# Output projections in two halves of 512 tokens, later half first in the even layer, and the first MLP iteration taken product by product

## The chip, the cores and the metric

The kernel runs on one core of one Trainium2 chip. The metric is the device time of one execution in microseconds (us), the median of the runs. The profiled execution is one more execution of the same program, with every instruction recorded.

## The reference

A two-layer decoder trunk, one batch of 1024 tokens, model width 1024, all in float32. Each layer is a mixer and an MLP, each inside a sandwich of two RMS norms with a modulation computed from `c`:

```
h   = rms_norm(x) * (1 + scale) + shift
x   = x + gate * rms_norm(mixer(h))          # even: Mamba-2 heads | differential attention
h   = rms_norm(x) * (1 + scale) + shift      # odd:  retention | sliding-window attention
x   = x + gate * rms_norm(relu(h @ W1)**2 @ W2)
```

`mixer(h)` ends in an output projection: the concatenated head outputs (2048 columns in the even layer, 1536 in the odd one) times a weight matrix with 1024 columns. This projection, the norms behind it, and the start of `h @ W1` are what the change rearranges.

## The kernel before

Every float32 product is made of three TensorE (PE) matmuls: each operand is split into a high part (written by a cast on ScalarE, ACT) and a low part (the difference, written by VectorE, DVE). In names, `wh`/`wl` are the two parts of a weight tile, `hh`/`hl` those of the normalized input `hT`, `uh`/`ul` those of a projected activation. `split_w` makes a weight pair: the cast at L160, the subtraction at L162. Instructions are put on each engine by a scheduler of the build, so program text gives the dependences and priorities and the scheduler the order; once built, each engine's order is fixed, and an instruction that waits holds back all behind it on its engine. DMAs go out from SP's queue.

The four sub-layers are numbered s = 0 (even mixer), 1 (MLP), 2 (odd mixer), 3 (MLP). Tokens are eight tiles of 128 (`t` = 0 to 7); a *half* is four tiles, 512 tokens.

**Output projection** (`MixerOut`). The mixer's columns are taken in groups of 512: four groups in the even layer, three in the odd one, listed in `order`. For one group, `half` transposes the activations of one half of the tokens (tile `pyt`, L922), scales them on ACT (L929) and splits them on DVE (L930). `load_group` loads the group's weights (two DMAs of 1 MB into `raw`), splits them into four pairs, and lets `bg` start one or more background tasks. `out_unit` (L456 to L458) is one token tile by 512 output columns: twelve 128x512 matmuls into a bank of `pg`, then a copy (L463, first group) or an addition (L465) into `Y` on DVE. `__init__` does the first half of the tokens for the first two groups, while the heads of the mixer are still being computed. `finish` did the rest: the second half for groups 1 and 0, then all eight token tiles of each remaining group, and with the last group also the norm and residual of each tile (`post`, L383 and L388), the norm of the next sub-layer (`pre_norm`, L372) and the transposes into `hT[0]` (`hT_cols`, L425 to L429).

**Background tasks** (`bg`, queue `bgq`): the modulation vectors of later sub-layers. A task loads a piece of the modulation matrix (`mraw`, into the same ring of two `raw` buffers as the weights) and accumulates it on DVE (`macc`, L289); four of these end in `parts` (L210, L211).

**Even mixer, end.** The last of eight attention heads is computed in blocks of 128 queries, from the last block to the first. A block goes through PE (`psc`, L857), DVE (L1215, bias and maximum), ACT (L1218, exponential), DVE (L1223 to L1228), PE (`pat`, L1235, transposes), ACT or DVE (L1237), PE (`pav`, L1241), ACT (L1245), DVE (L133), GpSimd (POOL, L135) and DVE (`ys`, L1248).

**MLP, first matrix** (`ud` is its result). The product of a 2x2 block form is made with seven products instead of eight (operands `A[1]` to `A[7]`, weights `x11` to `x22`, sums and differences of them). Each product is two times twelve matmuls (L547 to L549). Iteration 0 of eight starts as soon as `hT[0]` (the first half of the tokens) is there: products 1 and 2 need nothing else. `second_half` then makes the other operands from `Y[4]` to `Y[7]`: 32 transposes (L564), ACT (L566, L568, L500) and DVE (L501, L570 to L574); then come products 4, 6, 7, 5, 3.

## Time and profile before

| | us |
|---|---|
| median of 3 runs | 3018.76 (3018.48 to 3020.44) |
| profiled execution, its own time | 3018.32 |
| its span (first to last instruction) | 3016.5 |
| outside the span | 1.8 |
| PE busy in the span | 2922.7 |
| DVE busy | 1978.0 |
| ACT busy | 1325.2 |
| POOL busy | 471.9 |

The sub-layers follow each other in the span: the even mixer ends its attention near 957, its output projection near 1088, where the first MLP begins; the odd mixer ends its output projection near 2364, where the second MLP begins. The mean granted clock of PE over the span is 0.988 of full speed.

### The profile page before, as it was taken

Reading aid. Unit: us, or ns where it says so; the run is one execution under the profiler, and the core shown is the slowest. Engines: PE = TensorE matmul, PEld = TensorE weight load, DVE = VectorE, ACT = ScalarE, POOL = GpSimd, SP = SyncE. Lnnn points to the kernel's source line nnn. Section 1 sums busy time; section 2 is a strip of 40 time slices with the busy share of each in tenths; the row PEclk is TensorE's granted clock in tenths of the full one; section 3 lists DMA queues with packets and bytes.
Section 4 is the critical chain, followed back from the end, with each engine's and each line's share of the span. In section 5 each row is a group of like instructions: output and inputs, shape, how many; then the busy total and the mean of one; then the engine's idle time right before and its main releaser. Section 6 shows DMA issues by size and latency. Waiting matters only on the chain.

```text
span 3016.5 us, 40087 instructions
## 1 busy us (share of the span) xinstructions
PE 2922.7 (97%) x15250; PEld 2465.3 (82%) x15250; DVE 1978.0 (66%) x3211; ACT 1325.2 (44%) x2359; POOL 471.9 (16%) x430
## 2 busy tenths in 40 slices
PE   8999999999999989999999989999999899999998
PEld 5888888898877867888888878989988678888887
DVE  5677875765686579876646845565454876666476
ACT  5343335555553264445333545432222644454343
POOL 0244532322200020000000232001101200000021
PEclk9999999999999999999999999999999999999999
DMA  6211211322142236646736542153242464476464
GB/s 216 75 55 50 90 43 50 109 66 67 55 149 97 72 123 229 217 158 242 281 126 233 190 131 64 33 172 102 81 154 77 147 199 149 151 268 232 146 231 160
DMA packets 269091, 413.60 MB, mean 137 GB/s; under 512 B 15721, under 2 KB 151522, under 8 KB 268002
## 3 DMA queue, kind: packets, MB, share of 16 engines
q1 hardware_dynamic: 268512, 410.92, 40.0%
q8 instruction: 120, 1.97, 0.3%
q14 instruction: 73, 0.60, 0.1%
q10 hardware_dynamic: 386, 0.11, 0.0%
HBM read 319.23 MB, written 91.75 MB: 136 GB/s over the span
## 4 chain that ended last, share of the span: by engine, by line
PE 85%; DVE 6%; DMA 4%; ACT 2%; issue 1%; POOL 1%; SPq 0%; POOLq 0%; DVEq 0%; ACTq 0%
PE pg L444 5%; PE pg L445 5%; PE pg L446 5%; PE pw L730 5%; PE pw L731 5%; PE pw L732 5%; PE pw L547 4%; PE pw L548 4%; PE pw L549 4%; PE pg L798 4%; PE pg L800 4%; PE pg L799 4%; PE pg L456 3%; PE pg L458 3%; PE pg L457 3%; PE pg L730 2%
## 5 line engine op out<-in xcount | busy, mean ns | idle before, releaser
L160 ACT CAST wh<-raw 128x1024 fp32r<-128x1024 f32 (+1 forms) x218 | 227.4, 1047 | 331.0 <-PE pw L548 104.5
L798 PE MATMUL pg<-wh,hh 128*128 128x256 f32 (+1 forms) x992 | 290.7, 293 | 11.2 <-DVE ms L133 6.0
L444 PE MATMUL pg<-hh,wh 128*128 128x512 f32 x736 | 293.0, 398 | 3.4 <-ACT wh L160 2.5
L446 PE MATMUL pg<-hh,wl 128*128 128x512 f32 x736 | 292.1, 397 | 0.3 <-DVE ms L133 0.3
L162 DVE TENSOR_TENSOR wl<-raw,wh 128x1024 fp32r<-128x1024 f32 (+1 forms) x162 | 199.3, 1233 | 141.0 <-ACT wh L160 138.9
L445 PE MATMUL pg<-hl,wh 128*128 128x512 f32 x736 | 291.1, 396 | 0.0
L800 PE MATMUL pg<-wh,hl 128*128 128x256 f32 (+1 forms) x992 | 286.2, 289 | 0.6 <-DVE hl L429 0.6
L799 PE MATMUL pg<-wl,hh 128*128 128x256 f32 (+1 forms) x992 | 285.0, 287 | 0.0
L500 ACT CAST u<-uraw 128x1024 fp32r<-128x1024 f32 x112 | 117.0, 1049 | 298.4 <-PE pw L731 177.0
L501 DVE TENSOR_TENSOR u<-uraw,u 128x1024 fp32r<-128x1024 f32 x112 | 141.0, 1261 | 152.0 <-ACT u L500 151.7
L731 PE MATMUL pw<-wl,u 128*128 128x512 f32 x608 | 240.3, 395 | 0.0
L730 PE MATMUL pw<-wh,u 128*128 128x512 f32 x608 | 240.1, 396 | 0.0
L732 PE MATMUL pw<-wh,u 128*128 128x512 f32 x608 | 239.4, 394 | 0.0
L135 POOL TENSOR_TENSOR rs<-ms,expo 128x1 f32<-128x1 f32 x160 | 106.9, 669 | 642.4 <-DVE ms L133 630.2
L798 PEld LDWEIGHTS pg<-wh,hh 128*128 128x128 f32 x992 | 191.7, 193 | 14.3 <-issue 8.1
L799 PEld LDWEIGHTS pg<-wl,hh 128*128 128x128 f32 x992 | 191.6, 193 | 1.9 <-issue 0.5
L800 PEld LDWEIGHTS pg<-wh,hl 128*128 128x128 f32 x992 | 191.1, 193 | 2.0 <-DVE hl L429 1.3
L456 PE MATMUL pg<-wh,u 128*128 128x512 f32 x448 | 181.9, 406 | 2.7 <-DVE u L930 2.1
L458 PE MATMUL pg<-wh,u 128*128 128x512 f32 x448 | 178.3, 398 | 0.0
L457 PE MATMUL pg<-wl,u 128*128 128x512 f32 x448 | 177.0, 395 | 0.0
L162 POOL TENSOR_TENSOR wl<-raw,wh 128x1024 fp32r<-128x1024 f32 x58 | 145.9, 2520 | 155.6 <-ACT wh L160 148.6
L444 PEld LDWEIGHTS pg<-hh,wh 128*128 128x128 f32 x736 | 139.1, 189 | 31.8 <-ACT wh L160 2.9
(456 smaller groups left out, 7237.0 us busy)
## 6 DMA issues: line engine op xcount, KB each, us to landing
x<-in_mlp_w_dram SPq DMA_DIRECT2D x128, 512.0 KB, 7.5
uraw<-ud SPq DMA_DIRECT2D x56, 1024.0 KB, 5.6
mraw<-in_mod_w_dram SPq DMA_DIRECT2D x64, 512.0 KB, 4.6
ud<-sums SPq DMA_DIRECT2D x48, 512.0 KB, 5.3
raw<-in_mlp_w_dram SPq DMA_DIRECT2D x18, 1024.0 KB, 6.0
raw<-in_e_w_in_dram SPq DMA_DIRECT2D x32, 512.0 KB, 3.9
ud<-c SPq DMA_DIRECT2D x64, 256.0 KB, 3.0
raw<-in_mlp_w_dram SPq DMA_DIRECT2D x28, 512.0 KB, 5.0
```

The lines of the kernel that those rows point to most:

```text
L162: lo_on[0].tensor_tensor(out=wl, in0=src, in1=wh.bitcast(F32), op=ALU.subtract)
L444: mm(ps, lhsT=wh[:, k], rhs=hh[:, k], start=(k == 0), stop=False)
L445: mm(ps, lhsT=wh[:, k], rhs=hl[:, k], start=False, stop=False)
L446: mm(ps, lhsT=wl[:, k], rhs=hh[:, k], start=False, stop=(k == 7))
L456: mm(ps, lhsT=uh[:, tl], rhs=wh[:, f % 2], start=(f == 0), stop=False)
L458: mm(ps, lhsT=ul[:, tl], rhs=wh[:, f % 2], start=False, stop=(f == 3))
L730: mm(ps[t], lhsT=uh[:, k, ts], rhs=wh[:, k], start=b, stop=False, **on)
L731: mm(ps[t], lhsT=uh[:, k, ts], rhs=wl[:, k], start=False, stop=False, **on)
L732: mm(ps[t], lhsT=ul[:, k, ts], rhs=wh[:, k], start=False, stop=e, **on)
L798: mm(ps[:, 0:n], lhsT=hh[:, k, tl], rhs=wh[:, i], start=(k == 0), stop=False)
L799: mm(ps[:, 0:n], lhsT=hh[:, k, tl], rhs=wl[:, i], start=False, stop=False)
L800: mm(ps[:, 0:n], lhsT=hl[:, k, tl], rhs=wh[:, i], start=False, stop=(k == 7))
```

## The change

`out_group` is gone; `finish` does the projections by halves:

- For groups 2 and up, only the first half of the tokens; tokens outside, column halves inside. Then all background tasks that are left are issued (`bg(len(bgq))`).
- Then the second half for all groups, from the last group down to 0. Beside these units, one step of `along` at a time does `post`, `pre_norm` and `hT_cols` for the first half. With group 0, `post` and `pre_norm` follow for each tile of the second half.
- Weights of a group that is needed twice, at a distance, are loaded and split twice: seven calls of `load_group` in place of five in the even layer, five in place of four in the odd one.
- In the even layer the first half is tokens 512 to 1023 (`real(t)` gives the tile's place in memory); the odd mixer turns its halves round.
- The transposed activations of `finish` in the even layer go to the bank pool `pt` instead of `pg`.

In the MLP's iteration 0, `second_half` is a generator of five steps. Its first step is held behind the last matmul of product 2 by `tc.issue_after`; each later step makes the operand of the next product. The order of the products is 4, 7, 6, 5, 3. One quarter (`a21`) is transposed twice, so that 48 transposes are made instead of 32.

```diff
+            def group(i):
+                return load_group(self.w, self.order[i] * 512)
-            room = (pg, "g") if self.s == 0 else (pt, "t")
-            for i in (1, 0):
-                nc.sync.dma_start(out=yr[:, i], in_=self.yd[self.order[i]][:, 4:8])
-                us = self.half(i, 1, [yr[:, i, t] for t in range(4)], u_tiles(), *room)
-                if i == 0:
-                    bg_n[0] = 2
-                    self.gb = load_group(self.w, self.order[0] * 512)
-                for cc in range(2):
-                    for t in range(4, 8):
-                        out_unit(yp, [None, us], self.gb, t, cc, i == 1)
-            n = len(self.order)
             for i in range(2, n):
                 bg_n[0] = 5
-                us = [self.half(i, hf, [yr[:, hf * 4 + t] for t in range(4)], u_tiles(), pt, "t") for hf in range(2)]
-                gb = load_group(self.w, self.order[i] * 512)
-                late = out_group(yp, us, gb, self.s, False, i == n - 1)
+                us = self.half(i, 0, [yr[:, t] for t in range(4)], u_tiles(), pt, "t")
+                self.gb = group(i)
+                for t in range(4):
+                    for cc in range(2):
+                        out_unit(yp, [us, None], self.gb, t, cc, False)
+            bg(len(bgq))
...
+            for i in reversed(range(n)):
...
+                us = self.half(i, 1, [yr[:, i % 2, t] for t in range(4)], u_tiles(), pt, "t")
+                gb = self.gb if i == n - 1 else group(i)
+                for t in range(4, 8):
+                    for cc in range(2):
+                        out_unit(yp, [None, us], gb, t, cc, i == n - 1)
+                        if step % 2 == 0 or n == 3:
+                            along(step if n == 3 else step // 2)
+                        step += 1
+                    if i == 0:
+                        x_new = post(yp, t, s)
+                        if s != sub_last:
+                            pre_norm(yp, t, x_new)
```

```diff
                 for g in range(2):
-                    product(pa[g], 2, w, g, False, True)
+                    last = product(pa[g], 2, w, g, False, True)
                     square_relu(c11[g], pa[g])
-                if it == 0:
-                    second_half()
...
+                more = second_half() if it == 0 else iter(range(5))
+                with tc.issue_after(last):
+                    next(more)
                 for g in range(2):
                     product(pe[g], 4, w, g, True, True)
```

How the orders moved, at three places (line numbers below are those of the kernel that is shown in each).

First, PE near the end of the even mixer: the last blocks of the last attention head. `psc_8916` is the last block's score tile, `pat` and `pav` its transposes and its product with `v`; L456 to L458 (L463 to L465 in the changed kernel) are matmuls of `out_unit`. Before:

```order
L1241 MATMUL pav<-v,aT 128x128 [waits DVE_49]
L1241 MATMUL pav<-v,aT 128x128 x2
L1235 MATMUL pat<-kmat,p 128x128 [waits DVE_49]
L1235 MATMUL pat<-kmat,p 128x128
L857 MATMUL psc_8916<-ks,qh 128x128 [waits Activation_49]
L858 MATMUL psc_8916<-ks,ql 128x128
L457 MATMUL pg<-wl,u 128x512
L458 MATMUL pg<-wh,u 128x512
L456 MATMUL pg<-wh,u 128x512 [waits DVE_49]
L457 MATMUL pg<-wl,u 128x512
L458 MATMUL pg<-wh,u 128x512
```

After the change, from the same score tile to the first unit of the next group:

```order
L881 MATMUL psc_8916<-ks,qh 128x128 [waits Activation_49]
L882 MATMUL psc_8916<-ks,ql 128x128
L1303 MATMUL pav<-v,aT 128x128 [waits DVE_49]
L1303 MATMUL pav<-v,aT 128x128 x2
L1297 MATMUL pat<-kmat,p 128x128 [waits DVE_49]
L1297 MATMUL pat<-kmat,p 128x128
L1303 MATMUL pav<-v,aT 128x128 [waits Activation_49]
L1303 MATMUL pav<-v,aT 128x128
L1297 MATMUL pat<-kmat,p 128x128 [waits DVE_49]
L1303 MATMUL pav<-v,aT 128x128 [waits Activation_49]
L948 MATMUL pyt<-kmat,yr 128x128 [waits DMAHW5_49,DVE_49]
L948 MATMUL pyt<-kmat,yr 128x128 x3
```

The 96 matmuls of the eight units of group 1, second half, stood between the last blocks of the attention; they now stand after groups 3 and 2, and nothing but attention is left from the end of `__init__`'s units to the first `pyt` of group 2.

Second, DVE at the same place: the accumulations of the background task (`macc`), and the attention's pieces (L1215 before is L1277 after). Before, the last `ys` and the `macc` rows behind the attention:

```order
L162 TENSOR_TENSOR wl<-raw,wh 128x1024 [waits Activation_49]
L133 TENSOR_SCALAR ms<-ssd__8941 128x1 [waits Activation_49]
L930 SCALAR_TENSOR_TENSOR u<-pyt,cols,u 128x512 [waits Activation_49] x2
L1248 TENSOR_SCALAR ys<-pav,rs,rc 128x128 [waits DMAHW2_49,Pool_49]
L289 SCALAR_TENSOR_TENSOR macc<-mraw,cact,macc 128x1024 [waits DMAHW5_49]
L930 SCALAR_TENSOR_TENSOR u<-pyt,cols,u 128x512 [waits Activation_49]
L289 SCALAR_TENSOR_TENSOR macc<-mraw,cact,macc 128x1024 [waits DMAHW6_49,DVE_49]
```

After:

```order
L162 TENSOR_TENSOR wl<-raw,wh 128x1024 [waits Activation_49]
L133 TENSOR_SCALAR ms<-ssd__8691 128x1 [waits Activation_49]
L1299 COPY aT<-pat 128x256 [waits PE_49]
L1286 RECIPROCAL rc<-mx 128x1 [waits Activation_49]
L1310 TENSOR_SCALAR ys<-pav,rs,rc 128x128 [waits DMAHW2_49,Pool_49]
L289 SCALAR_TENSOR_TENSOR macc<-mraw,cact,macc 128x1024 [waits DMAHW5_49]
L1277 ISA psc_8802,mx<-psc_8802,bt_3966 128x512 [waits PE_49]
L1277 ISA mx 128x1
L1277 ISA psc_8842,mx<-psc_8842,bt_3966 128x384
L1277 ISA mx 128x1
L289 SCALAR_TENSOR_TENSOR macc<-mraw,cact,macc 128x1024 [waits DMAHW6_49,DVE_49]
```

The four `macc` rows and L211 stood behind the attention; they now stand among it, ahead of the blocks from `psc_8802` to `psc_8916`.

Third, ACT at the start of the first MLP's iteration 0: `xt` is the residual of a token tile, `wh` and `t` weights of the products, `p` the copy of product 1 (L607 before, L605 after). Before:

```order
L427 ACTIVATE hh_10331<-pht,b_9511,a_9510 128x512 [waits PE_49]
L428 ACTIVATE whole<-pht,b_9511,a_9510 128x512
L160 CAST wh<-raw 128x1024 [waits DVE_49]
L160 CAST wh<-t_10723 128x1024
L160 CAST wh<-raw 128x1024 [waits DMAHW2_49,PE_49]
L370 ACTIVATE junk,ss_10502<-xt 128x1024 [waits DVE_49,Activation_49]
L607 COPY p_10530<-pg 128x512
L607 COPY p_10531<-pw 128x512 [waits PE_49]
```

After:

```order
L377 ACTIVATE junk,ss_10495<-xt 128x1024 [waits DVE_49,Activation_49]
L387 ACTIVATE junk,ss<-Y 128x1024 [waits DVE_49,Activation_49]
L377 ACTIVATE junk,ss_10545<-xt 128x1024 [waits DVE_49,Activation_49]
L160 CAST wh<-raw 128x1024 [waits DVE_49,PE_49]
L160 CAST wh<-raw 128x1024 [waits DMAHW0_49,PE_49]
L160 CAST wh<-t_10640 128x1024 [waits PE_49]
L605 COPY p_10573<-pg 128x512
L605 COPY p_10574<-pw 128x512 [waits PE_49]
```

The activations that make `hT[0]` (L427, L428) are gone from ACT's queue here, since they ran during the projections; the squares of the last two token tiles (`ss_10495`, `ss_10545`) stand ahead of the casts and of the copy of product 1.

## Rows read from the trace of the kernel before

**Rows 1.** The page: busy time of the engines; the chain that ended last, by engine.

```profile
PE 2922.7 (97%) x15250; PEld 2465.3 (82%) x15250; DVE 1978.0 (66%) x3211; ACT 1325.2 (44%) x2359; POOL 471.9 (16%) x430
...
PE 85%; DVE 6%; DMA 4%; ACT 2%; issue 1%; POOL 1%; SPq 0%; POOLq 0%; DVEq 0%; ACTq 0%
```

**Rows 2.** Stretches, all engines: length, busy time (instructions) of each, clock, DMA.

```profile
core 0: us, PE busy (x) PEld busy (x) DVE busy (x) ACT busy (x) POOL busy (x), PEclk, DMA share, GB/s
915.00:955.00 40.00, 39.66 (x226) 34.09 (x225) 25.60 (x70) 15.13 (x43) 3.31 (x6) 1.00 0.05 13
955.00:970.00 15.00, 10.69 (x44) 8.10 (x44) 11.79 (x16) 6.15 (x9) 0.55 (x1) 0.77 0.53 167
1085.00:1135.00 50.00, 38.19 (x176) 30.42 (x175) 44.83 (x66) 38.42 (x61) 6.52 (x6) 0.90 0.38 126
1135.00:1150.00 15.00, 11.60 (x48) 8.58 (x47) 15.00 (x18) 4.51 (x7) 0.00 (x0) 1.00 0.45 137
2364.00:2405.00 41.00, 31.47 (x142) 25.01 (x141) 37.24 (x55) 31.59 (x51) 3.13 (x4) 0.83 0.36 120
2405.00:2420.00 15.00, 11.62 (x49) 8.53 (x48) 14.96 (x20) 4.28 (x5) 0.00 (x0) 1.00 0.49 164
```

**Rows 3.** PE's timeline, even tail: start, duration, operation [idle before, its releaser].

```profile
924.09 0.40 PE L458 MATMUL pg<-wh,u 128*128 128x512 f32 x1
...
954.60 0.39 PE L458 MATMUL pg<-wh,u 128*128 128x512 f32 x1
954.83 0.39 PE L456 MATMUL pg<-wh,u 128*128 128x512 f32 x1
...
964.01 0.79 PE L456 MATMUL pg<-wh,u 128*128 128x512 f32 x1 [2.14 <-DVE u L930]
```

**Rows 4.** DVE's timeline, even tail, same columns.

```profile
956.79 1.23 DVE L162 TENSOR_TENSOR wl<-raw,wh 128x1024 fp32r<-128x1024 f32 x1 [1.76 <-ACT wh L160]
...
958.53 1.22 DVE L162 TENSOR_TENSOR wl<-raw,wh 128x1024 fp32r<-128x1024 f32 x1
...
962.01 1.28 DVE L289 SCALAR_TENSOR_TENSOR macc<-mraw,cact,macc 128x1024 f32<-128x1024 f32 x1 [0.56 <-DMA mraw<-in_mod_w_dram]
...
966.18 2.61 DVE L289 SCALAR_TENSOR_TENSOR macc<-mraw,cact,macc 128x1024 f32<-128x1024 f32 x2 [0.38 <-DMA mraw<-in_mod_w_dram]
```

**Rows 5.** DVE by line, 915 to 975: count, busy, mean ns, idle before.

```profile
L289 DVE SCALAR_TENSOR_TENSOR macc<-mraw,cact,macc 128x1024 f32<-128x1024 f32 x4 | 5.1, 1283 | 1.0 <-DMA mraw<-in_mod_w_dram 0.9
L162 DVE TENSOR_TENSOR wl<-raw,wh 128x1024 fp32r<-128x1024 f32 x4 | 4.9, 1222 | 2.3 <-ACT wh L160 2.3
L1215 DVE CUSTOM_DVE_ANT_0 psc<-psc,bt 128x512 f32<-128x512 f32 (+4 forms) x9 | 4.6, 544 | 1.3 <-PE psc L858 1.3
L1228 DVE SCALAR_TENSOR_TENSOR p<-p,rc 128x640 f32<-128x640 f32 (+4 forms) x5 | 3.1, 616 | 0.1
L1248 DVE TENSOR_SCALAR ys<-pav,rs,rc 128x128 f32<-128x128 f32 x7 | 2.8, 406 | 2.2 <-POOL rs L135 2.2
```

**Rows 6.** PE's timeline where the first MLP begins.

```profile
1088.02 0.39 PE L458 MATMUL pg<-wh,u 128*128 128x512 f32 x1
...
1109.65 0.78 PE L547 MATMUL pg<-hh,wh 128*128 128x512 f32 x1
1110.22 0.63 PE L548 MATMUL pg<-hl,wh 128*128 128x512 f32 x1
1110.65 0.63 PE L549 MATMUL pg<-hh,wl 128*128 128x512 f32 x1
...
1122.89 1.03 PE L564 MATMUL pht<-kmat,Y 128*128 128x128 f32 x8
```

**Rows 7.** DVE's timeline at the same place.

```profile
1105.36 1.22 DVE L162 TENSOR_TENSOR wl<-t,wh 128x1024 fp32r<-128x1024 f32 x1
1106.49 1.22 DVE L162 TENSOR_TENSOR wl<-raw,wh 128x1024 fp32r<-128x1024 f32 x1
```

**Rows 8.** ACT's timeline at the same place.

```profile
1102.50 1.06 ACT L160 CAST wh<-raw 128x1024 fp32r<-128x1024 f32 x1
1103.45 1.07 ACT L370 ACTIVATE junk<-xt 128x1024 bf16<-128x1024 f32 x1
1104.50 0.58 ACT L607 COPY p<-pg 128x512 f32<-128x512 f32 x1
```

More of the change, by code (lines that the diff above doesn't have):

```diff
@@ L642, in mlp @@
                     square_relu(u3[g], u3[g])
+                if it == 0:
+                    next(more)
                 w = split_w(shape, x22)
@@ L960, in finish @@
-            return yp, late
+                yr = hp.tile([P, 4, 512], F32, tag=("hl1", "hh0")[i % 2], name="yr")
+                nc.sync.dma_start(out=yr, in_=self.yd[self.order[i]][:, real(0):real(0) + 4])
+                us = self.half(i, 0, [yr[:, t] for t in range(4)], u_tiles(), pt, "t")
[4 more added lines that the diff above has]
+            bg(len(bgq))
@@ new lines, in finish, with along @@
+            xs, k_at = {}, [0]
+            def along(step):
+                if step < 4:
+                    xs[step] = post(yp, step, s)
+                if 1 <= step < 5 and s != sub_last:
+                    pre_norm(yp, step - 1, xs[step - 1])
+                if step == 5 and s != sub_last:
+                    hT[0] = new_hT(0)
+                    yp.whole = None
+                    if s % 2 == 0:
+                        pairs = [slot(17 + i, [P, 2, 512], F32, "whole") for i in range(3)]
+                        pairs.append(const.tile([P, 2, 512], F32, tag="macc", name="whole"))
+                        yp.whole = [t[:, i] for t in pairs for i in range(2)]
+                if step >= 6 and s != sub_last and step < 14:
+                    hT_cols(yp, 0, s + 1, hT[0], (step - 6,), yp.whole)
@@ new lines, in finish @@
+            step = 0
+            for i in reversed(range(n)):
+                if (n - 1 - i) % 2 == 0:
+                    yr = hp.tile([P, 2, 4, 512], F32, tag="hl1", name="yr")
+                    for j in range(i, max(i - 2, -1), -1):
+                        nc.sync.dma_start(out=yr[:, j % 2], in_=self.yd[self.order[j]][:, real(4):real(4) + 4])
+                us = self.half(i, 1, [yr[:, i % 2, t] for t in range(4)], u_tiles(), pt, "t")
[10 more added lines that the diff above has]
+                            pre_norm(yp, t, x_new)
```

162 lines of the change are left out of this document (89 added, 73 removed).

## The prediction

> **What bounds the kernel now.** I read the page first. PE is busy 2922.7 of 3016.5 us and makes up 85% of the chain that ended last [rows 1]. A change of order can therefore only win or lose in the stretches where PE stands still, so next I listed the stretches of the span in which PE's busy time falls short [rows 2]. Around the change there are four. The end of the even mixer, 955 to 970, has 10.7 us of PE in 15; the start of the first MLP 38.2 in 50, then 11.6 in 15; the start of the second MLP 31.5 in 41, then 11.6 in 15. Between 915 and 955 PE is full (39.7 of 40). The reader should see in the same rows that DVE is what is nearly always busy there: 44.8 of 50 and 15.0 of 15 at the first MLP, 11.8 of 15 at the tail. In these stretches PE waits for DVE's queue, directly or through ACT, and that queue's order is what the change alters. Then I read the timelines of PE, DVE and ACT at those places [rows 3, 4, 6 to 8].
>
> Two paces are needed. At full clock a 128x512 matmul starts 0.23 us after the one ahead of it [rows 3]; at the lower of the clock's two levels (1.2 GHz), 0.43 [rows 6]. DVE's 1024-wide operations last 1.22 and follow at 1.13, so 0.09 of a duration lies over the next [rows 7].
>
> **What is lost today.** At the tail: 4.3 us of PE idle [rows 2]; at 964.01 PE resumes after a wait for `u` [rows 3], and the lower clock costs about ten matmuls 0.2 each, 2.0; with some overlap at the gaps, about 7. At the first MLP the last unit ends at 1088.25 and product 2 starts at 1109.65 [rows 6], 21.4 later. PE's own work in between is product 1 (24 x 0.23 = 5.6) and 24 transposes (eight take 1.03 with the pipeline's end, so 0.11 each: 2.6); 13.2 is lost. Twelve slow matmuls behind it lose 12 x 0.2 = 2.4, and 3.4 is idle in 1135 to 1150 [rows 2]. Sum 19.0. The second MLP reads alike, a little less idle at a lower mean clock (0.83 for 0.90) [rows 2]; I take 18.7.
>
> **The change, part by part.**
>
> *The even tail, +13.* Today the 96 matmuls of group 1's second half (96 x 0.23 = 22 us) lie between the last attention blocks, which is why 915 to 955 is full [rows 2]. They move behind groups 2 and 3. The last unit of `__init__` ends at 924.3 today [rows 3]; without the attention matmuls that stand ahead of its last four, at about 923. From there to the first `pyt` the new PE order holds 45 transposes and small products and eight score matmuls, and with two `pyt` tiles about 8 us of work. How long that takes is decided by DVE, whose new order puts four `macc` and L211 in the midst of it.
> The first `macc` needs a matrix piece that can only be loaded when a weight buffer is free. That takes a cast (1.06, [rows 8]) and an L162 (1.22) from 923, so 925.2. Today the buffer is free at 956.79 + 1.23 = 958.02 and the piece is there at 962.01 [rows 4], 4.0 later; so 929.2. The second pair comes 6.4 after its buffer today (959.75 to 966.18, [rows 4]), thus about 933.3, just when its turn comes. Behind the first `macc` stand, by [rows 5]: four `macc` at 1.28 (5.1), L211 (like L162, 1.2), seven L1215 at 0.54 (3.8), four L1228 at 0.62 (2.5), six `ys` at 0.41 (2.4), three copies (taken as 0.55, 1.7) and 24 one-column operations at about 0.15 (an estimate: 3.6). That is 20.3, less 0.09 for each of 49 hand-overs: 15.9, so 945. The way from there (last block, `yr`'s load, `pyt`, ACT) adds about 4 by my estimate, since some of it runs beside DVE: first unit near 949. Idle is 949 - 923 - 8 = 18, and the slow restart costs 2 again. 20 against 7 is +13. Bounds: if the pieces are early or DVE is not held by them, `macc` and L211 still take some 6 or are out of the way altogether. Without them DVE's 14 us end at 938, the first unit is at 942, and the loss 13 (+6); if the last block and the load take 3 us more, +16.
>
> The wait for the piece holds back everything behind it on DVE's queue, and with it the last blocks' PE and ACT work. The Trainium skill ("PSUM — Partial Sum Buffer", section "Engine vs sequencer instructions") says that VectorE's queue is strictly first in, first out; with that the tail costs +13, and if later DVE work could pass the waiting `macc` it would be the lower bound, +6. The trace agrees so far: in [rows 4] the `macc` stand idle 0.56 and 0.38 us for the DMA, in order.
>
> *The start of each MLP, -4.4 and -4.1.* `hT[0]` is now finished under the second half's units, so product 1 starts at once when the last unit ends (T0), and 16 transposes with their ACT work leave the stretch. But product 2 accumulates on the bank that `COPY p` reads, and ACT reaches that copy only after three casts, and these only after the square of the last residual tile; that is new in ACT's order. The residual is made on DVE behind: an L162 of product 1 (to T0 + 1.1), the last addition (0.6), a weight difference (1.13), `yg` (0.6), `Y` (0.66), two weight differences (2.26) and the residual itself (1.2), with the small ones T0 + 7.8 (paces by [rows 7], 512-wide ones at half). ACT then takes 1.05 for the square (1103.45 to 1104.50), three casts at 0.95 and the copy, 0.58 [rows 8]: T0 + 12.3, with the second copy and the hand-overs 13. PE has 5.6 to do, so 7.4 is lost (13.2 before). The slow restart stays, 2.4. What follows is like today's 3.4, as the operands are still made one behind the other by ACT and DVE; I take 3. The 16 extra transposes cost 16 x 0.11 = 1.8. Sum 14.6 against 19.0 and 18.7. Bounds: if the scheduler's queues run so that the copy comes right behind product 1, the loss is 3 + 1.8 (-14 each); if the steps of the generator are each waited for (their ACT and DVE work is 1 to 2 us a step, four steps), 18, -1 each.
>
> *Switches of weights, +3.* With tokens outside, all four weight pairs of a group are in use until its last two units, 5.5 us (24 x 0.23). The next group's first pair needs one cast and one L162, 2.3 together, after its buffer is free about 4 us before the end; it just fits if ACT and DVE are free, and `along` now gives them squares and residuals there. I take 0.5 for each of four switches in the even and three in the odd layer, with 0 and 1.2 as bounds (0 to 8). The three extra weight loads (each four casts and four L162, 9 us of ACT and DVE together, and 2 MB) fall into stretches of about 115 us in which PE is the bound; they cost nothing unless they are late for a switch, which is that term.
>
> *No price:* `real(t)`, the turned halves, and the other PSUM pool change no count of instructions. The odd mixer's own tail keeps its order, so 0, give or take 2.
>
> **Sum.** 13 - 4.4 - 4.1 + 3 = +7.5 on the profiled execution's 3018.3: 3025.8. The median of the runs stands 0.4 above the profiled one, so 3026.
>
> **The rivals.**
> (a) *The starts are covered as the change is meant.* Product 2 comes right behind product 1, PE meets no slow restart, and each MLP gains 14; with the tail at +6 to +13 and switches at +3 the sum is -12 to -19, at 3000 to 3007. For it: `hT[0]` is ready, all 48 matmuls stand together in PE's order. Against it: ACT's order puts the square of the last tile ahead of the copy, and DVE was busy 44.8 of 50 us there [rows 2]. It decides when `COPY p` starts before T0 + 8.
> (b) *The background task doesn't hold the attention.* Tail +6, the rest as forecast: +0.5, 3019. For it: 915 to 955 has 14 us of free DVE [rows 2]. Against it: the new order and the 4.0 us load.
> (c) *Every switch waits.* If the casts of the next group are late by 1.5 to 2 us each, seven switches give 10 to 14: 3033 to 3037. For it: ACT's in-order queue now holds `along`'s squares; against it, ACT is busy under half the time.
> (d) *Nothing net.* Gains and losses meet within 6 us, above all when the starts gain 8 each: 3018.
> (e) *A second fall of the clock.* 16 transposes in a row stand behind product 2. If PE's clock fell there, 12 more slow matmuls each, +4.8 in all: 3031. [rows 6] speak against it: at 1122.89 eight transposes stand among matmuls and the pace behind them is not the slow one. The Trainium skill ("TensorE: Matmul & The Clock Gate", "Part 4: PE-mode transpose") says that transposes don't count as busy like matmuls do, which would make it likelier.
>
> **How the numbers follow.** The forecast 45% (its own range 3016 to 3034), (a) 20%, (b) 12%, (c) 10%, (d) 8%, (e) 5%. No change is told from a change within 0.2%, 6.0 us: faster is below 3012.7, slower above 3024.8. Slower: 30 of the forecast's 45, (c) and (e): 45%, and 2 of (d) and (b). Faster: (a), and 3 of the others. The range from 3005 to 3038 leaves out the lower part of (a) and the upper end of (c).
>
> **What would show it.** Right: in the new profile PE is mostly idle between 923 and 949, with the first `macc` near 929 ahead of L1277 rows; the MLP's first 24 matmuls run without a gap, then PE waits some 7 us for ACT's L605, whose predecessor on ACT is the square of the last tile. Wrong: a tail with a first unit before 942, a product 2 that follows within 3 us, or waits of PE for L160 or L162 over 1 us at each switch.

## The result and the profile after

The changed kernel takes 3053.01 us, the median of four runs (3050.33 to 3056.16), against 3019.07 for the kernel before. The recorded ratio is 1.0105, 95% interval 1.0093 to 1.0117 (the quotient of these two medians, 1.0112, lies inside it). It is slower, as forecast, but by 34 us and not by 7; the time lies outside the predicted range. The profiled execution took 3054.58, 36.3 more than that of before. The page of the changed kernel, its span and busy times, answering to [rows 1]:

```profile
span 3052.8 us, 40231 instructions
...
PE 2944.3 (96%) x15282; PEld 2480.1 (81%) x15282; DVE 1989.5 (65%) x3224; ACT 1343.5 (44%) x2378; POOL 473.3 (16%) x430
```

PE is busy 21.6 us longer, though the change adds only 32 transposes to it (3.5 us at 0.11): most of the rest is work done at the lower clock, whose mean fell from 0.988 to 0.982 (busy time times mean clock grows by 3.7 only). The other 14.7 us of the 36.3 are idle time. To see where, I cut the span at three points that both kernels have: the first matmul of product 1 of each MLP (T0, T1) and the first transpose of the odd mixer (O). Each stretch is the difference of two start times in PE's timeline.

| | start to T0 | T0 to O | O to T1 | T1 to end |
|---|---|---|---|---|
| before | 1088.25 | 653.77 | 619.15 | 655.33 |
| after | 1100.64 | 657.70 | 632.08 | 662.38 |
| difference | +12.4 | +3.9 | +12.9 | +7.1 |
| without the moved transposes | +10.6 | +5.7 | +11.2 | +8.8 |

The last row allows for 16 transposes (1.75 us) that stood behind T0 and T1 before and stand ahead of them now. So the even tail cost 10.6, the two MLP starts 5.7 and 8.8, where a gain was forecast, and the odd mixer 11.2, where nothing was.

The first stretch holds some 870 us that the change doesn't touch. So that these don't count as tail, I take a point just ahead of it: six `pav` matmuls of the last head, which both kernels have. In PE's timeline of before, and of the changed kernel with the first matmul of the next unit:

```profile
921.95 0.83 PE L1241 MATMUL pav<-v,aT 128*128 128x128 f32 x6
```

```profile
921.54 0.83 PE L1303 MATMUL pav<-v,aT 128*128 128x128 f32 x6
...
950.26 0.78 PE L463 MATMUL pg<-wh,u 128*128 128x512 f32 x1
```

From there to T0 it is 166.3 before and 179.1 after, 12.8 more, or 11.0 without the moved transposes. The 10.6 is the tail's indeed.

The same stretches in the windows of all engines, answering to [rows 2] (columns as there):

```profile
915.00:955.00 40.00, 30.29 (x147) 24.05 (x146) 26.82 (x67) 15.71 (x43) 3.84 (x7) 0.79 0.44 143
955.00:970.00 15.00, 14.53 (x69) 11.71 (x69) 8.95 (x15) 2.43 (x4) 0.00 (x0) 1.00 0.56 211
1098.00:1138.00 40.00, 29.73 (x133) 22.63 (x132) 27.45 (x35) 23.79 (x37) 4.65 (x4) 0.87 0.29 98
1138.00:1163.00 25.00, 18.90 (x73) 14.30 (x72) 25.00 (x37) 10.81 (x17) 0.00 (x0) 0.86 0.40 140
1800.00:1820.00 20.00, 14.12 (x53) 11.17 (x53) 6.55 (x12) 6.09 (x11) 5.14 (x4) 0.83 0.38 112
970.00:1098.00 128.00, 127.86 (x603) 104.42 (x602) 79.02 (x118) 53.74 (x76) 25.03 (x25) 1.00 0.37 128
```

Between 915 and 955, full before, PE now misses 9.7 us and its clock falls to 0.79. At the MLP start the shortage has moved back: 1138 to 1163 has DVE busy without a break and PE with 18.9 of 25. The row at 1800 is a place that the prediction never looked at, in the odd mixer. The last row is the even projection from 970 to just ahead of T0, with the whole second half in it: no switch of weights is waited for.

PE's timeline of the changed kernel at the first MLP start (products 1 and 2, then what precedes products 4 to 6), answering to [rows 6]:

```profile
1100.64 0.40 PE L522 MATMUL pw<-hh,wh 128*128 128x512 f32 x1
...
1115.15 0.79 PE L522 MATMUL pg<-hh,wh 128*128 128x512 f32 x1 [8.68 <-ACT p L605]
...
1150.80 0.50 PE L523 MATMUL pg<-s,wh 128*128 128x512 f32 x1 [1.88 <-DVE s L476]
...
1154.94 0.80 PE L522 MATMUL pg<-hh,wh 128*128 128x512 f32 x1 [2.94 <-DVE p L627]
```

The forecast wait on ACT's `COPY p` is there, 8.68 us against 7.4, and product 2 starts 14.5 behind T0 against 13. Behind it stands what was not forecast: waits for DVE's low parts and sums, 1.88 and 2.94 where before had 1.2 at the most, and at 1154.94 a second slow restart (the first matmul behind a wait is 0.80 long at the lower level and 0.50 at the higher; the next ones are 0.63 and 0.40).

DVE's timeline of the changed kernel, in the tail and, in the last row, at the MLP start, answering to [rows 4, 5]:

```profile
926.69 1.28 DVE L289 SCALAR_TENSOR_TENSOR macc<-mraw,cact,macc 128x1024 f32<-128x1024 f32 x1 [1.07 <-DMA mraw<-in_mod_w_dram]
...
949.87 0.75 DVE L956 SCALAR_TENSOR_TENSOR u<-pyt,dn,u 128x512 fp32r<-128x512 f32 x1 [0.43 <-ACT u L955]
...
1110.37 1.22 DVE L614 TENSOR_TENSOR raw<-raw,t 128x1024 f32<-128x1024 f32 x1
```

The first `macc` waits for its matrix piece and starts at 926.69 (forecast 929), in the midst of the attention's work; the first activations for the next unit are split at 949.87, and its first matmul is the one at 950.26 above (forecast 949). ACT's timeline around the copy that product 2 waits for, answering to [rows 8]:

```profile
1110.55 1.06 ACT L377 ACTIVATE junk<-xt 128x1024 bf16<-128x1024 f32 x1 [5.37 <-DVE xt L395]
...
1111.68 1.99 ACT L160 CAST wh<-raw 128x1024 fp32r<-128x1024 f32 x2
1113.58 1.04 ACT L160 CAST wh<-t 128x1024 fp32r<-128x1024 f32 x1
1114.53 0.58 ACT L605 COPY p<-pg 128x512 f32<-128x512 f32 x1
```

The order is the forecast one: residual, square, three casts, copy. But two things end at the same moment ahead of the casts: the square at 1111.61 and, on DVE, L614 at 1111.59, the weight difference that the first cast reads. Which of them held the copy can't be read here.

### The profile page after: what moved, and what is told of

Read it like the earlier page. It is cut to its first block, busy times and chain, and to the rows that moved or that the text cites. A ratio compares the mean times of both kernels' runs of the same rounds, so it can differ in the third digit from the quotient of the medians.

```text
span 3052.8 us, 40231 instructions
## 1 busy us (share of the span) xinstructions
PE 2944.3 (96%) x15282; PEld 2480.1 (81%) x15282; DVE 1989.5 (65%) x3224; ACT 1343.5 (44%) x2378; POOL 473.3 (16%) x430
## 4 chain that ended last, share of the span: by engine, by line
PE 62%; DVE 3%; ACT 1%; DMA 1%; issue 1%; POOL 0%; POOLq 0%; SPq 0%; ACTq 0%
PE pw L754 5%; PE pw L755 5%; PE pw L756 5%; PE pw L523 4%; PE pw L522 4%; PE pw L524 4%; PE pg L463 3%; PE pg L464 3%; PE pg L465 3%; PE pg L522 2%; PE pg L523 2%; PE pg L754 2%; PE pg L524 2%; PE pg L755 2%; PE pg L756 2%; PE pg L822 2%
## 5 line engine op out<-in xcount | busy, mean ns | idle before, releaser
L160 ACT CAST wh<-raw 128x1024 fp32r<-128x1024 f32 (+1 forms) x230 | 239.6, 1047 | 321.8 <-PE pw L523 99.3
L162 DVE TENSOR_TENSOR wl<-raw,wh 128x1024 fp32r<-128x1024 f32 (+1 forms) x174 | 211.5, 1220 | 149.8 <-ACT wh L160 134.7
L822 PE MATMUL pg<-wh,hh 128*128 128x256 f32 (+1 forms) x992 | 291.4, 294 | 11.2 <-DVE ms L133 6.3
L822 PEld LDWEIGHTS pg<-wh,hh 128*128 128x128 f32 x992 | 192.2, 194 | 14.3 <-issue 8.3
L463 PE MATMUL pg<-wh,u 128*128 128x512 f32 x448 | 181.7, 406 | 1.7 <-DVE Y L472 0.5
L465 PE MATMUL pg<-wh,u 128*128 128x512 f32 x448 | 176.8, 397 | 0.0
```

The lines of the kernel that those rows point to most:

```text
L162: lo_on[0].tensor_tensor(out=wl, in0=src, in1=wh.bitcast(F32), op=ALU.subtract)
L463: mm(ps, lhsT=uh[:, tl], rhs=wh[:, f % 2], start=(f == 0), stop=False)
L822: mm(ps[:, 0:n], lhsT=hh[:, k, tl], rhs=wh[:, i], start=(k == 0), stop=False)
```

## The experiments

Ratios are to the kernel before on the same chip, in five rounds, with 95% intervals. The stretches are those of the table above. "Start to T0" is not compared between experiments: it holds some 870 us that no kernel touches and that differ by some microseconds among the profiles; the tail is compared by windows and from the `pav` row to T0. The last stretch is less sure than the others: e4, e7, e8 and the changed kernel have the same MLP code and lie between 660.41 and 662.38.

| kernel | ratio | T0 to O | O to T1 | T1 to end |
|---|---|---|---|---|
| e1_no_pin | 1.0072 [1.0059, 1.0085] | 654.70 | 629.66 | 656.91 |
| e2_mlp_before | 1.0019 [1.0010, 1.0027] | 645.77 | 632.01 | 648.72 |
| e3_mlp_after_alone | 1.0029 [1.0017, 1.0042] | 658.91 | 620.23 | 662.53 |
| e4_square_on_dve | 1.0100 [1.0086, 1.0114] | 657.37 | 632.09 | 660.95 |
| e5_copy_first | 1.0057 [1.0043, 1.0071] | 651.23 | 629.12 | 654.17 |
| e6_fill | 1.0056 [1.0043, 1.0068] | 656.88 | 629.07 | 660.71 |
| e7_background_late | 1.0082 [1.0069, 1.0094] | 657.72 | 629.80 | 660.41 |
| e8_k_order | 1.0085 [1.0071, 1.0098] | 657.95 | 625.60 | 661.34 |
| e9_by_blocks | 1.0063 [1.0050, 1.0075] | 652.00 | 628.61 | 654.44 |
| e10_fill_order_mlp | 0.9983 [0.9973, 0.9992] | 646.61 | 622.05 | 655.47 |
| e11_and_copy_first | 1.0017 [1.0009, 1.0026] | 652.38 | 619.30 | 657.44 |
| e12_and_square | 1.0001 [0.9992, 1.0010] | 647.94 | 623.99 | 652.66 |
| e13_product_order | 1.0025 [1.0015, 1.0035] | 645.92 | 632.75 | 648.43 |
| e14_fill_and_late | 0.9984 [0.9975, 0.9993] | 646.40 | 621.33 | 653.64 |

**The two halves of the change apart: e2 and e3.** e2 has the new projections with the MLP code of before (32 transposes, all operands made at once, products 4, 6, 7, 5, 3); e3 has the old projections with the new MLP code. The core of e2's edit:

```diff
-                more = second_half() if it == 0 else iter(range(5))
-                with tc.issue_after(last):
-                    next(more)
+                if it == 0:
+                    second_half()
```

> New projections, but the whole MLP code of the kernel before (second_half in one piece, 32 transposes, order 4, 6, 7, 5, 3). P and Q both say that the waits behind product 2 shrink to the 3.4 us of before, some 5 us less at each MLP, and 1.8 less for 16 transposes: 3038 to 3042. R says that the 8 to 9 us at the start stay, since the square, the casts and the copy stand on ACT as before. If new projections alone made the starts worse, the total stays above 3046.

> Projections of the kernel before, MLP code of the changed one. If the MLP part alone costs what the trace of the changed kernel shows at the two MLPs (+5 and +8 us against before), 3030 to 3034, and 915 to 970 and the odd mixer's start read as before. If it is the two parts together that cost (hT[0] ready early makes the pin matter), 3016 to 3024.

With the old MLP code the new projections gain at each start: 645.77 against 653.77 (-8.0), and 648.72 against 655.33 (-6.6). Of each, 1.75 is the transposes that moved ahead of the start, so 6.2 and 4.8 are gained. The new MLP code in the old projections loses at each: +5.1 and +7.2. So the projections do at the starts what they could be expected to do, and the new iteration 0 takes more than all of it back.

**Which part of the new MLP code: e13, e9, e1.** They are steps from e2 to the changed kernel. e13 is e2 with the products in the order 4, 7, 6, 5, 3. e9 has the new code, without the pin, and makes the operands block by block as before. e1 is the changed kernel without the pin, its generator in five steps.

```diff
  e1:
-                with tc.issue_after(last):
-                    next(more)
+                next(more)
  e9, besides:
                 for k in range(4):
...
-                yield
-                for k in range(4):
                     tt(out=a11[k], in0=a21(k), in1=a11[k], op=sub)
...
+                for _ in range(5):
+                    yield
```

> The changed kernel without the pin: the first step of the MLP's operands may go ahead of product 2. Theory P (the pin is what costs): in the changed kernel DVE stands idle 7.2 us at each MLP start while product 2 runs, because the transposes come only behind it, and pays for it 25 us later (PE waits 1.3, 1.9 and 2.9 us for DVE near 1146 to 1155, then a slow restart). Without the pin these later waits go: 8 us less at each of the two MLPs, some 16 less in all, about 3037. Rival Q (the work itself: 48 transposes, five steps and the order 4, 7, 6, 5, 3 keep ACT and DVE busy longer than the products last): the later waits stay within 2 us, total 3049 to 3054. Rival R (ACT's queue: the copy of product 1 behind the square of the last tile): the wait of 8.7 us ahead of product 2 stays in both cases.

> The kernel without the pin, with the same 48 transposes, the same products in the order 4, 7, 6, 5, 3, but the operands made block by block (for each of four blocks all its sums and splits) instead of step by step. Theory S: what is left of the loss at the MLP starts without the pin (21 us each against 14 with the MLP code of before) comes from the step order: the first step is four tiles of transposes with two ACT passes each and one short DVE operation, so DVE works 6 of the first 15 us behind product 2's start (11 to 13 in before's order) and is then full for 20 us with PE waiting. Then DVE is busy from the start, and each MLP start loses 14 to 16: 10 to 14 us less than without the pin, a ratio near 1.003. Rival X: the 16 extra transposes with their ACT passes and the product order are what costs; then no more than 4 us less than without the pin, 1.006 to 1.0075.

> New projections with the MLP code of before (32 transposes, operands made in one piece), but iteration 0's products in the changed kernel's order 4, 7, 6, 5, 3. The run by blocks differs from it by the 16 extra transposes and their ACT passes alone, the run with the MLP of before by the order alone. If the order of the products costs: MLP starts near 18 us each, ratio near 1.004. If the extra transposes and their ACT passes cost: starts near 14, ratio 1.001 to 1.0025, as with the MLP of before.

Step by step, T0 to O and T1 to end: the order of the products +0.2 and -0.3 (e13 against e2), nothing; the new operand code, 48 transposes with one more ACT pass a block, +6.1 and +6.0 (e9 against e13), of which PE's own time for 16 transposes is 1.8; the operands in five steps and not block by block +2.7 and +2.5 (e1 against e9); the pin +3.0 and +5.5 (the changed kernel against e1). None of these steps gains. e9 differs from e13 not in the transposes alone: it also keeps `a21` in a PSUM bank, builds the sums in another order and in other buffers, and writes them out in smaller DMAs. The 6.1 belongs to all of this together.

Why the pin doesn't help is in PE's longest waits at the first MLP start, in us in total, times and longest. e1:

```profile
PE pht L542 <- DVE Y L379: 6.0, 1, 6.0
PE pg L523 <- DVE s L476: 3.2, 2, 1.9
PE pg L522 <- DVE p L626: 2.9, 1, 2.9
PE pg L522 <- ACT p L605: 1.0, 1, 1.0
```

and e2:

```profile
PE pht L539 <- DVE Y L379: 6.0, 1, 6.0
PE pw L522 <- DVE p L602: 1.1, 1, 1.1
PE pw L523 <- DVE s L476: 1.1, 1, 1.1
PE pg L522 <- ACT p L582: 1.0, 1, 1.0
```

Without the pin, PE makes eight transposes before product 2; it waits 6.0 in front of one of them for the last residual and 1.0 for the copy; product 2 starts at 1117.62, 14.3 behind T0. With it, it starts 14.5 behind T0. The copy holds product 2 back either way, and the pin only takes the transposes out of a wait that is there anyhow and puts them behind it. Behind product 2 a wait of 1.2 for ACT (L555) is then new, which e1 doesn't have. This is what the pin costs at the first start: 0.2 on product 2, 0.9 for the eight transposes (at 0.11) and 1.2 for the wait, together 2.3 of the 3.0. It is not work of DVE or ACT that the wait loses. From T0 to product 2, the changed kernel and then e1:

```profile
1100.64:1115.15 14.51, 5.83 (x25) 4.24 (x23) 13.20 (x17) 6.82 (x11) 3.94 (x3) 0.81 0.35 130
```

```profile
1103.32:1117.62 14.30, 6.99 (x32) 4.98 (x30) 12.99 (x17) 6.61 (x11) 3.94 (x3) 0.82 0.35 129
```

At the second start the waits read the same; of the 5.5 there, up to 2.0 is the spread of the last stretch, and the rest is not explained.

The other waits, 3.2 and 2.9, don't come with the pin, as theory P had it, since e1 has both. Most of the first comes with the five steps, and of the second about 1: e9 has 0.5 and 1.8, e13 1.1 and 1.2. What DVE does in the first 15 us behind product 2 follows the same steps. The changed kernel's windows, in pieces of 5 us from product 2's start, and then where PE starves:

```profile
1115.15:1120.15 5.00, 5.00 (x12) 3.97 (x13) 1.62 (x2) 0.44 (x1) 0.00 (x0) 0.53 0.00 0
1120.15:1125.15 5.00, 3.80 (x22) 3.03 (x20) 1.22 (x1) 3.52 (x6) 0.00 (x0) 1.00 0.14 52
1125.15:1130.15 5.00, 4.93 (x25) 3.70 (x26) 2.09 (x4) 5.00 (x8) 0.00 (x0) 1.00 0.74 242
1145.15:1150.15 5.00, 2.50 (x12) 1.55 (x10) 5.00 (x9) 3.50 (x7) 0.00 (x0) 1.00 0.69 216
1150.15:1155.15 5.00, 1.41 (x5) 0.89 (x6) 5.00 (x8) 1.57 (x2) 0.00 (x0) 0.88 0.50 203
```

and the 15 us behind product 2 in e1, in e9 and in e2:

```profile
1117.62:1132.62 15.00, 15.00 (x63) 12.28 (x64) 6.31 (x9) 10.51 (x17) 0.00 (x0) 0.83 0.28 89
```

```profile
1117.35:1132.35 15.00, 15.00 (x64) 12.21 (x64) 9.89 (x14) 10.85 (x18) 0.00 (x0) 0.84 0.29 94
```

```profile
1115.38:1130.38 15.00, 15.00 (x63) 12.29 (x64) 13.11 (x20) 12.96 (x22) 0.00 (x0) 0.83 0.28 90
```

DVE does 4.93 us of work in these 15 us in the changed kernel, 6.31 without the pin, 9.89 without the five steps too, and 13.11 in e2. So 1.4 of the 8.2 that are missing go with the pin, 3.6 with the steps and most of the rest with the operand code (e13, which has only the order of the products changed, has 12.94). What is not done there is missing 30 us later, where DVE is full and PE has 3.91 us of work in 10.

**What holds the copy: e4 and e5.** e4 makes the square of the last tile on DVE, so that ACT need not wait for it ahead of the casts. e5 has that too, and puts the casts of products 4, 6 and 7 behind the copy on ACT.

```diff
  e4 (t == 7):
-        nc.scalar.activation(junk, xsrc, AF.Square, accum_out=ss)
+        nc.vector.tensor_tensor_reduce(out=junk, in0=xsrc, in1=xsrc, scale=1.0, scalar=0.0,
+                                       op0=ALU.mult, op1=ALU.add, accum_out=ss)
  e5, besides:
-                    nc.scalar.copy(out=p1[g], in_=pa[g])
+                    copied = nc.scalar.copy(out=p1[g], in_=pa[g])
...
+                def behind():
+                    return tc.issue_after(copied.ins) if it == 0 else ExitStack()
...
-                w = split_w(shape, x21)
+                with behind():
+                    w = split_w(shape, x21)
```

> The changed kernel, with the square of each sub-layer's last token tile taken on DVE instead of ACT, so that the casts and the copy of product 1 don't stand behind it. R: the wait ahead of product 2 falls from 8.7 us to 3 or 4 at both MLPs, everything behind it moves up: 8 to 12 us less in all, about 3042. If DVE is what sets the start (its queue is full until 12 us behind the last unit), the wait moves elsewhere and the total stays within 4 us of 3053.

> The changed kernel with two edits in the MLP's iteration 0: the square of the last token tile on DVE (as in the run before, which moved nothing), and the three weight casts of products 4, 6 and 7 held behind the copy of product 1 on ACT. Theory C: product 2 waits 8.7 us because the copy stands on ACT behind casts whose source (L614, a weight difference for product 4) DVE makes only 11 us behind the last unit. Then product 2 follows product 1 within 1 us, PE has no slow restart there, the pinned transposes come some 8 us earlier, and each MLP's start gains 8 to 11 us: 16 to 22 less than the changed kernel, a ratio to before near 1.004. Rival: DVE's weight differences and residual set the pace anyway; then the wait appears behind product 2 (PE waiting for Y or for L555 and L476), and the gain is under 6 us.

e4 changes nothing (1.0100 against 1.0105). ACT's timeline of e4:

```profile
1117.64 1.99 ACT L160 CAST wh<-raw 128x1024 fp32r<-128x1024 f32 x2 [6.50 <-DVE raw L618]
...
1120.49 0.58 ACT L609 COPY p<-pg 128x512 f32<-128x512 f32 x1
```

With no square ahead of them the casts wait 6.50 us for the weight difference (L618 here, L614 in the changed kernel) in DVE's queue. The copy comes 13.9 behind T0 (1106.60), as in the changed kernel (1114.53 - 1100.64 = 13.9). In e5, with the casts behind the copy, the wait of 8.7 is gone from PE's list of waits:

```profile
PE pg L527 <- DVE s L480: 3.1, 2, 1.9
PE pg L526 <- DVE p L636: 2.9, 1, 2.9
...
```

Product 2 follows product 1 at full clock, 5.7 behind T0, and the starts give back 6.5 and 8.2. The 3.1 and 2.9 stay. So the copy was held by the casts, and these by DVE's queue; the square was one of two equal holders. (e11 below has the casts behind the copy and the square still ahead of it, and there PE waits 5.7 for the copy.) The Trainium skill ("PSUM — Partial Sum Buffer", section "Engine vs sequencer instructions") calls ScalarE's queue strictly first in, first out; the pair e4 and e5 agrees, since the copy needs nothing from the casts and yet came only behind them and their 6.5 us of waiting.

**The tail: e6 and e7.** e6 puts the second half of group 1 back between the last attention blocks, with the weights still there from `__init__`; the later second-half pass leaves that group out, and `along`'s steps are spread over the fewer units. e7 starts no background task with the groups of `finish`; all are issued behind them.

```diff
  e6:
+            us = self.half(1, 1, [yr[:, t] for t in range(4)], u_tiles(), *((pg, "g") if s == 0 else (pt, "t")))
+            for cc in range(2):
+                for t in range(4, 8):
+                    out_unit(yp, [None, us], self.gb, t, cc, True)
             for i in range(2, n):
...
-            for i in reversed(range(n)):
+            seq = [i for i in reversed(range(n)) if i != 1]
+            for q, i in enumerate(seq):
  e7:
-                bg_n[0] = 5
+                bg_n[0] = 0
```

> The changed kernel, but group 1's second half is projected first, as before the change (its weights are still there, so two calls of load_group fewer), and the second-half pass is over groups 3, 2, 0 (2, 0 in the odd layer). Theory T (the tail is the lost filler of 22 us of matmuls, together with the macc rows among the attention): 915 to 970 loses some 8 us again instead of 20, so about 10 to 12 less than the changed kernel: a ratio near 1.007. If the macc rows alone hold the attention, whatever filler there is, the tail stays within 4 us of the changed kernel's.

> The changed kernel with no background task issued by the weight loads of groups 2 and 3; all that are left come behind them (one number changed, bg_n 5 to 0). This is the macc part of the tail by itself. By the sum of the prediction, first unit near 942 instead of 949 and a gain of 6 to 7 us, a ratio near 1.0085. If the attention's own chain (ACT, POOL, PE in turn) sets the tail without filler, the gain is under 3 us; the macc then appear later and may delay the first post, where PE is the bound and nothing is lost.

Windows of e6:

```profile
915.00:955.00 40.00, 39.79 (x232) 34.38 (x231) 25.17 (x68) 16.12 (x43) 3.29 (x6) 1.00 0.20 63
955.00:970.00 15.00, 11.11 (x49) 8.80 (x48) 8.90 (x16) 4.55 (x9) 1.06 (x2) 0.77 0.44 145
970.00:985.00 15.00, 12.62 (x58) 9.76 (x58) 11.13 (x16) 3.23 (x5) 0.00 (x0) 1.00 0.74 283
```

and of e7:

```profile
915.00:955.00 40.00, 33.74 (x181) 27.21 (x181) 24.79 (x68) 16.73 (x45) 4.28 (x7) 0.91 0.49 170
955.00:970.00 15.00, 15.00 (x68) 12.22 (x67) 6.60 (x9) 3.88 (x5) 0.00 (x0) 1.00 0.01 2
```

With the units back, 915 to 955 is as full as before, and the gap at its end is before's own [rows 2] with 2.4 us more behind it. From the `pav` row (927.26) to T0 e6 takes 168.0: 11.1 less than the changed kernel, and as long as before but for the moved transposes, though the `macc` still stand among the attention. Without `macc` in the attention (e7), PE has 48.7 us of work in the 55 where the changed kernel has 44.8. The first activations are split at 942.58 in e7, against 949.87, and the first unit starts at 942.71, 7.5 us earlier: the prediction's lower bound had 942. But part of it is lost again, since the tasks that were put off cost PE 2.4 us between 970 and 1094 (121.48 busy, 123.86 in the changed kernel), and from the `pav` row (921.75) to T0 it is 176.7: 2.4 gained. So the missing units are what makes the tail. The `macc` hold the attention only where the units are gone, and where they are back, putting the tasks off gains 0.4 (168.1 in e14 against 168.5 in e10, both below). That e7's ratio came out as expected is in part luck: by the profiles 4.2 of its 6.4 us lie behind T0, 2.3 of them in the odd mixer, where its clock stayed up (see the end).

**The odd mixer: e8.** In the changed kernel the late half of the odd mixer's tokens comes first in the projection of k and v. e8 takes the early half first again.

```diff
-            proj_fm(w, 3584, 1, k_both)
+            proj_fm(w, 3584, 1, k_both, hfs=(early, 1 - early))
...
```

> The changed kernel, with the two first projections of the sliding-window part (L1397 and the next) taken in the order of the halves in which hT becomes ready (the early half first), as the order was before the halves were turned round. Theory O: at 1805 PE waits 5.9 us for L1395 because both halves of the first projection end together, one of them waiting for the late half, and both PSUM banks are given back late. Then the wait falls to 1 us and the slow restart behind it goes: 7 to 8 less, a ratio near 1.008. If the turned halves cost elsewhere (late load of far, DVE queue), the wait stays.

PE's waits at the start of the odd mixer, the changed kernel:

```profile
PE pg L822 <- DVE ms L133: 6.3, 1, 6.3
PE pg L451 <- DVE ks L1395: 5.9, 1, 5.9
```

and e8:

```profile
PE pg L822 <- DVE ms L133: 6.2, 1, 6.2
PE pg L451 <- DVE ks L1395: 0.8, 1, 0.8
```

O to T1 falls from 632.08 to 625.60, by 6.5, and before too the second wait was 0.8 long. In PE's timeline of the changed kernel the units of both halves run side by side and end together near 1805; by my reading both banks of `pg` are then given back only when DVE has worked through `ks`, and the next projection waits.

**Put together: e10, e14, e11, e12.** e10 is e6 with e8's order and the MLP code of before. e14 is e10 with e7's late tasks. e11 is e10 with the casts behind the copy, as in e5, and `second_half` behind product 2; e12 is e11 with e4's square on DVE.

```diff
  e11, against e10:
-                    second_half()
+                    with tc.issue_after(last):
+                        second_half()
...
+                with behind():
+                    w = split_w(shape, x21)
```

> Three findings together: group 1's second half first (filler), the sliding-window projections in order of readiness, and the MLP code of before. From the regions of the single runs: tail 8, odd mixer's start 7, MLP starts 20 and 3.5 for the transposes, all less than the changed kernel's +34; two weight loads fewer count nothing on PE. Expected 5 less than before (-3 to -12), a ratio of 0.996 to 0.999. If the gains of filler and order overlap with the waits that the other runs still had, it stays at 1.000 to 1.002.

> The fastest kernel so far (filler, order of the sliding-window projections, MLP of before), with the background tasks behind the weight loads of groups 2 and 3 as in the run that moved them late. If the macc rows still hold the tail where the filler is back, 2 to 4 us less than without this edit, a ratio of 0.997 to 0.998. If the filler hides them, the same ratio (0.998 to 0.999).

> As the run before, and in the MLP's iteration 0 the three later casts behind the copy of product 1, and the transposes (32, in one piece) behind product 2. Theory C and S together: product 2 starts when the square of the last tile is done on ACT, 2 to 3 us earlier than in the run before, and not behind the transposes of the last tile; each MLP start gains 3 to 6: a ratio of 0.993 to 0.996. If DVE's weight differences set the pace anyway, no difference to the run before.

> As the run before, and the last tile's square on DVE. Then the copy stands behind nothing that is late: product 2 follows product 1 within 1 us, no slow restart before the transposes; each MLP start gains another 3 to 5 unless PE then waits for the last tile's transposes by the same amount (the residual is ready 10 us behind the last unit, DVE's queue decides): a ratio of 0.990 to 0.995, or as the run before.

e10 beats both kernels, by 0.17% of before's time: 0.9983 [0.9973, 0.9992], and e14 the same. It gains 7.2 at the first MLP start (5.4 without the moved transposes), but nothing at the second (655.47 against 648.72 in e2). PE's list of waits there has the reason in e10:

```profile
PE pht L539 <- DVE Y L379: 11.0, 2, 6.0
```

In e2 this is 6.0 in one wait. With a group fewer in the odd layer's second half, the last transposes for `hT[0]` come 6.2 us ahead of T1 (2356.55 for 2362.73), where e2 has them 31.6 ahead. The residuals of the second half stand behind this work on DVE, and 5.0 us more are waited for. e11 loses too: T0 to O is 652.38 against 646.61, and PE still waits 5.7 for the copy. It joins two edits, so this doesn't show which of them costs. Both e11 and e12 missed what was expected of them (0.993 to 0.996 and 0.990 to 0.995): an early product 2 did not add to the other gains. Why e12, with the square on DVE too, only gets back to 647.94 was not followed further.

## Why the prediction was right in sign and wrong in size

**The even tail, +13: right.** The first unit came at 950.26 for 949, `macc` at 926.69 for 929, in the place foreseen; the stretch cost 10.6. e6 and e7 show both halves of the reason, the missing units and the `macc`, and e7's first unit lands on the lower bound's 942. Only the path behind it was missed: of the 7 that the bounds give to `macc`, 2.4 are left at T0. Rival (b) is out, and (d) with the result.

**The start of each MLP, -4.4 and -4.1: wrong, by 10.1 and 12.9.** This is the step that failed, and in it the term "What follows is like today's 3.4 ... I take 3". The first wait was right in place and size, 8.7 for 7.4. Its cause was only half named: e4 shows that without the square the casts wait as long for DVE. What follows was not like today: behind product 2 PE's waits at the first start sum to 7.6 (1.2, 0.3, 3.2 and 2.9) where 3 was taken, and a second slow restart, some 2.4 (twelve matmuls at 0.43 for 0.23), was not in the sum at all. e13, e9, e1 and the changed kernel price the reasons: 6.1 for the new operand code, where 1.8 was forecast for its transposes, 2.7 for operands made in five steps, 3.0 to 5.5 for the pin. I had the pin as free because product 2 waits anyway; but without it eight transposes stand ahead of product 2, and behind it they cost PE their own time and a wait for ACT. The pin takes no work of DVE and ACT out of the wait: from T0 to product 2 they do 13.2 and 6.8 us with it, 13.0 and 6.6 without (e1). DVE's 8 us of missing work come behind product 2, mostly from the steps and the operand code, and are missing when PE needs them. The bound from which I argued, "1 to 2 us a step", would have given -1 each; it took each step by itself and not the sum of a queue that starts late.

**The rivals on the starts.** Rival (a) names a true gain: with the MLP code of before the new projections do bring 6.2 and 4.8 (e2), less than half of its 14 each. The other half of the change spends it. Rival (e) didn't happen as told: from 1120.15 to 1130.15, where transposes stand among the matmuls behind product 2, the granted clock was 1.00 (the windows above). The Trainium skill ("TensorE: Matmul & The Clock Gate", "Part 4: PE-mode transpose") says that transposes don't count as busy like matmuls; mixed with matmuls, as here, they didn't lower the clock. A second fall came, at 1155, but behind waits of 1.9 and 2.9.

**Switches of weights, +3: nothing.** (Seven at 0.5 are 3.5; the sum has 3.) PE is busy 127.86 of 128 between 970 and 1098, and in the odd projection its waits from 2255 to 2391 are for activations and additions, none for weights, 1.2 at the most. Rival (c) is out as well.

**"No price": wrong for the turned halves.** They cost 6.5 (e8), by banks given back late. I had counted instructions, found none added, and looked no further; the order of the two halves within a ring of two banks was the thing to ask about. Of the other 4.7 in the odd mixer, about 3 is a lower clock (below) and the rest wasn't traced.

On the profiled execution the sum of +7.5 against +36.3 is so made up: the tail with the switches 5.4 less than forecast, the starts 23.0 more, the odd mixer 11.2 more.

Open: within the 6.1 for the new operand code, the runs don't separate ACT's extra passes from the PSUM banks that are held longer and from the other order of the sums. At the second start, 3.5 to 5.5 for the pin is more than its waits explain. e10 keeps less than its parts promise; 5.0 of that is the wait shown, the rest isn't placed.

## What to carry to other kernels

Work that is pinned behind a wait is not free because the engine waits there: ask what it did in that wait before, and what will now stand behind it. When operands are made "just in time" for each product, look at the engine that makes them: if it is the fullest one in the stretch, as DVE here, what it doesn't do early is missing late (here, 30 us later). And a change that only turns an order round can have a price where a ring of two buffers is filled by both sides of that order.

## What the hardware showed beside

Nearly the same short idle time lowered the clock in one kernel and not in another. In the last part of the odd projection PE waits nearly as before, three times, 2.7 us together against 2.5, and has 2.34 busy us in 5 against 2.55. The changed kernel's windows:

```profile
2260.00:2265.00 5.00, 2.34 (x15) 1.63 (x13) 4.25 (x9) 2.14 (x6) 0.55 (x1) 0.83 0.96 335
2265.00:2270.00 5.00, 5.00 (x18) 4.32 (x18) 2.08 (x3) 1.76 (x3) 0.00 (x0) 0.50 0.89 347
```

and before's:

```profile
2235.00:2240.00 5.00, 2.55 (x17) 1.74 (x17) 4.78 (x9) 2.67 (x6) 0.55 (x1) 1.00 0.88 305
2240.00:2245.00 5.00, 5.00 (x33) 4.33 (x32) 2.56 (x6) 2.53 (x5) 0.00 (x0) 1.00 1.00 411
```

After the wait the changed kernel runs at 0.50 (1.2 GHz) and starts 18 matmuls and transposes in 5 us where before starts 33. e8 fell too, to 0.50 in that place; e5 and e7 stayed at 1.00. It is worth about 3 us: a matmul behind the wait follows at 0.43 in place of 0.23. Nothing in these rows says beforehand which way it goes.
